# Adaptive-norm products: 28 of 36 streamed pieces move from TensorE to VectorE

## The chip, the cores and the metric

The kernel runs on one core of a Trainium2 chip. The metric is the device time of one execution in microseconds; the time before is the median of three runs.

## The reference, cut to what matters

The model is a two-layer trunk over 640 tokens (128 of context, 512 latent) with 1024 channels. Each layer first derives six modulation vectors of 1024 values from a conditioning vector, once for the context tokens (`c_ctx`) and once for the latent tokens (`c`):

```python
def adaln(cvec, w, b):
    m = jax.nn.silu(cvec) @ w + b          # (1024,) @ (1024, 6144)
    return jnp.split(m[:, None, :], 6, axis=-1)
...
sh1, sc1, g1, sh2, sc2, g2                  # the six parts, 0 to 5, in this order
h  = rmsnorm(x, g_norm1) * (1 + sc1) + sh1  # four mixers read h
x  = x + g1 * merged
h2 = rmsnorm(x, g_norm2) * (1 + sc2) + sh2
x  = x + g2 * (square(relu(h2 @ w_fc1)) @ w_fc2)
```

The rest of a layer (an SSD mixer, an S5 mixer, differential attention, windowed attention, gates, an output projection) is not touched by the change.

## The kernel before, in words

The activations stand transposed, channels on the 128 partitions and the 640 tokens along the free axis, in two halves of 320 tokens. A large product is split into three float32r products (high by high, low by high, high by low: lines 222, 223 and 224), so a dense block of 1024 inputs by 128 outputs takes 24 matrix products of 320 columns for each half. `load_w` brings a 512-column panel of weights (buffer `wr`, four slots), ScalarE copies it to its high part `wh` (line 211), and VectorE or, every third time, GpSimd subtracts to make the low part `wl` (line 195). The PSUM buffer of a dense half is `dn`, two slots. In the first product of the feed-forward block (`w_fc1`) ScalarE applies the ReLU (line 1742) and VectorE multiplies by `dn` again (line 1743), which frees the slot; in `w_out` and `w_fc2` VectorE adds the half to `x` (line 1537).

A modulation piece is a pair (part, q): 256 of the 6144 outputs. `adaln` computes it on TensorE: eight float32 products with the 32-column conditioning tile `cpad` as stationary operand and 256 columns of `w_mod` moving (line 287, each of them two records in the trace), four of them into each row group of one PSUM tile; a ScalarE copy to `mrow` (line 292); four products with `sel` that add the row groups and transpose (line 294); and one VectorE addition of the bias into `mods` (line 297). `make_gsc` (lines 341, 342) makes the gain of a norm out of part 1 or part 4.

Layer 0's parts 0, 1 and 2 are made in the prologue (buffers `wm`). The other 36 pieces are streamed by `adaln_ahead`, which loads each piece as four blocks of 256 KB into the ring `wa` (eight slots of 512 columns) and gives its products a higher scheduling priority. Layer 0's parts 3 and 4 (eight pieces) run in the output projection `w_out` of layer 0 (`PLAN["ad_out"]`). The rest is a generator `bgen` stepped by `between()`, five steps for every eight dense blocks of layer 0's feed-forward block: part 5 of layer 0 (four pieces), parts 0 and 1 of layer 1 (eight), the S5 matrices of layer 1 (`s5_build`, nine steps), parts 2 to 5 of layer 1 (sixteen). Layer 1's feed-forward block has no background work. The mid norm (`norm` with `PLAN["mid"]`) stands between `w_out` and `w_fc1`; its factor is a chain of small VectorE operations (`rsqrt`, lines 173 to 185), and its application is line 388 and line 400.

A scheduler orders the instructions of each engine and queue at build time with a simulated timeline; on the chip each engine and queue runs its list in that order. All `wr` and `wa` loads are issued by the SP queue.

Of the kernel before, what the change touches and what calls it, by code (L numbers as in the profile page):

```python
# [13 lines left out]
F32 = mybir.dt.float32  # L14
# [3 lines left out]
AF = mybir.ActivationFunctionType  # L18
ALU = mybir.AluOpType
# [4 lines left out]
D = 1024  # L24
# [18 lines left out]
NTAIL = 3  # L43

RINGS = dict(
    t1=3, tx=4, tq=6, ty=2, tw=5, td=5, nt=4, wa=8, wr=4, wh=4, wl=4, fh=10,
)

ENG = dict(
# [26 lines left out]
def hybrid_body(ctx: ExitStack, tc: tile.TileContext, a: dict, o: dict, dbg: dict):  # L76
    nc = tc.nc
    sp = nc.sync
# [7 lines left out]
    dp = ctx.enter_context(tc.tile_pool(name="dp", bufs=1, space=DRAM))  # L86
# [50 lines left out]
    def ring(tag, cols, where="pool"):  # L137
        def get(shape, name, dt=F32):
            n = int(np.prod(shape[1:]))
            t = top[where].tile([128, cols], dt, tag=tag, name=nm(name), bufs=RINGS[tag])[:, :n]  # L140
            if len(shape) == 2:
                return t
            letters = "abcdef"[: len(shape) - 1]
            dims = dict(zip(letters, shape[1:]))
            return t.rearrange(f"p ({' '.join(letters)}) -> p {' '.join(letters)}", **dims)

        return get
# [3 lines left out]
    t1, tx, tq = ring("t1", 320), ring("tx", 652), ring("tq", 256)  # L151
    ty, tw, td = ring("ty", 1024, "right"), ring("tw", 648, "right"), ring("td", 640, "right")

    nt, wa = ring("nt", 320), ring("wa", 512)

    def big(shape, tag, dt=F32, bufs=1, where="pool"):

        return top[where].tile(list(shape), dt, tag=tag, name=nm(tag), bufs=bufs)
# [116 lines left out]
    nc.vector.tensor_scalar(out=csg, in0=cth, scalar1=0.5, scalar2=0.5, op0=ALU.mult, op1=ALU.add)  # L275
    nc.vector.tensor_tensor(out=cpad[:, :, 0:2], in0=cs, in1=csg, op=ALU.mult)

    def adaln(l, parts, q, acc, out, raw, ks=range(KT)):

        n = len(parts)
        for i, part in enumerate(parts):
            for n_, k in enumerate(ks):
                r0 = 32 * (k % 4)
                c0 = (k % 2) * 256
                nc.tensor.matmul(  # L287
                    acc[r0:r0 + 32, i * 256:i * 256 + 256], cpad[:, k, :], raw(part, k // 2)[:, c0:c0 + 256],
                    start=(n_ < 4), stop=(n_ >= 4),
                )  # L290
        row = big([128, 512], "mrow", bufs=2) if n > 1 else t1([128, 256], "mrow")
        nc.scalar.copy(out=row, in_=acc[:, :n * 256])
        for j in range(2 * n):
            nc.tensor.matmul(out[:, 2 * j:2 * j + 2], row[:, j * 128:(j + 1) * 128], sel, start=True, stop=True)
        for i in range(n):
            f0 = parts[i] * 8 + q * 2
            nc.vector.tensor_tensor(
                out=mods[l][:, f0:f0 + 2, :],
                in0=out[:, 4 * i:4 * i + 4].rearrange("p (f s) -> p f s", s=2),
                in1=bmod[l][:, f0:f0 + 2].unsqueeze(2).to_broadcast((128, 2, 2)),  # L300
                op=ALU.add,
            )

    def adaln_ahead(l, parts, after=()):

        for part in parts:
            for q in range(4):
                halves = {}

                def raw(part, n, q=q, halves=halves):  # L310
                    if n not in halves:
                        halves[n] = wa([128, 512], "wa")
                        sp.dma_start(
                            out=halves[n], in_=a["w_mod"][l, part * 4 + q, n // 2][:, (n % 2) * 512:(n % 2) * 512 + 512]
                        )
                    return halves[n]


                for n in range(KT // 2):
                    raw(part, n)  # L320
                acc = mx()
                with tc.high_priority(offset=VISIT):
                    adaln(l, [part], q, acc[:, 0], acc[:, 1], raw, range(KT)[::-1])
                if q == 3 and part in after:
                    make_gsc(l, after[part])
                yield
# [8 lines left out]
    mods = [const(f"mod{l}", [128, 48, 2]) for l in range(L)]  # L335
# [137 lines left out]
    def s5_build(l, where, after):  # L473
# [114 lines left out]
            return x32[:, g0:g0 + 4].unsqueeze(2).to_broadcast((128, 4, n))  # L588

        def cmul(out, xr, yr, xi, yi, op, shape):  # L590
            u, v = big(shape, "s5u", bufs=2, where=where), big(shape, "s5v", bufs=2, where=where)
            nc.vector.tensor_tensor(out=u, in0=xr, in1=yr, op=ALU.mult)
            nc.gpsimd.tensor_tensor(out=v, in0=xi, in1=yi, op=ALU.mult)
            nc.vector.tensor_tensor(out=out, in0=u, in1=v, op=op)
# [964 lines left out]
    with tc.tile_pool(name="pro", bufs=1, reuse_waits="tile") as pool:  # L1559
        top["pool"] = pool  # L1560
        x = big([128, KT, T], "x")
        acc_n = big([128, T], "acc_n")
        h = h_tiles("h")

        accs, rb = mx(), mx()
        us = [big([128, 8, NI], "us0", bufs=2) for _ in range(2)]
        evs = [s5_store(u) for u in us]
        sums = [[dn(), dn()], [pb1(), None]]
        ws = []

        def panel_adaln(parts, q, acc, out):
            w = {part: [big([128, 1024], "wm", bufs=WM) for _ in range(2)] for part in parts}
            for part in parts:
                for i in range(2):
                    sp.dma_start(out=w[part][i], in_=a["w_mod"][0, part * 4 + q, i])
            if soon:
                load_all(soon)
                soon.clear()
            adaln(0, parts, q, acc, out, lambda part, n: w[part][n // 2][:, (n % 2) * 512:(n % 2) * 512 + 512])

        for q in range(5):
            if q < 4:
                panel_adaln((0, 1), q, accs[:, q % 2], rb[:, 0, HF + 8 * q:HF + 8 * q + 8])
                make_gsc(0, 0, 2 * q, 2)
            if q == 0:
                for k in range(KT):
                    sp.dma_start(out=x[:, k], in_=x_d[:, k])
                    for hf in range(2):
                        square_into(acc_n, x, k, hf)
                for hf in range(2):  # L1590
                    norm_spread(norm_factor(acc_n, hf)[0], rb, hf)
                sums[1][1] = pa()
                norms = [norm_mod(0, 0, x, rb, hf, *h) for hf in range(2)]
                continue
            for hf in range(2):
                step(norms[hf], 2)
            if q < 3:
                ws.append(load_ws(a["w_u"][0, q - 1], ahead=0))
            for k in {2: range(4), 3: range(4, 6), 4: range(6, 8)}.get(q, ()):
                for w, ps in zip(ws, sums):  # L1600
                    for hf in range(2):
                        mm3_step(ps[hf][:, :HF], split_w(w, k), hsl(h, k, hf), k == 0, k == KT - 1)
        for ev, ps, u, d in zip(evs, sums, us, u_d):
            for hf in range(2):
                ev(hf, ps[hf][:, :HF])
            nc.scalar.dma_start(out=d, in_=u)
        accs = mx()
        for q in range(4):
            panel_adaln((2,), q, accs[:, 0, (q % 2) * 256:], accs[:, 1, 8 * q:8 * q + 8])
        load_all(late)  # L1610
        maskf = t1([128, 2, 128], "mask")
        sp.dma_start(out=maskf, in_=a["wmask"])
        nc.vector.tensor_copy(out=maskb, in_=maskf)
        nc.vector.tensor_copy(out=identb, in_=ident)
        build_after[0] = h[1][0:1, KT - 1, T - 1:T].bitcast(F32)
        step(s5gen)
        adgen = adaln_ahead(0, range(3, 6), {4: 1})

    for l in range(L):
        acc_d = [dp.tile([128, T], F32, name=f"acc{l}_{f}") for f in range(KT)]  # L1620
# [92 lines left out]
        with ExitStack() as mlp:  # L1713
# [44 lines left out]
                )  # L1758

            norm(l, 1, x, acc_n, *h2, PLAN["mid"], tail, head)  # L1760
            bgen = [adgen]
            if l + 1 < L:
                bgen += [
                    adaln_ahead(l + 1, (0, 1), {1: 0}),
                    s5_build(l + 1, "mlp", lambda: act0[7][1][0:1, 0, T - 1:T].bitcast(F32)),
                    adaln_ahead(l + 1, range(2, 6), {4: 1}),
                ]
            bgen = itertools.chain(*bgen)

# [50 lines left out]
def _col(v):  # L1820

    v = np.asarray(v)
    return np.swapaxes(v.reshape(v.shape[:-1] + (v.shape[-1] // 128, 128)), -1, -2)


def _pack(inp):
# [3 lines left out]
    for n, s in sizes.items():  # L1830
# [9 lines left out]
    p = {}  # L1840
    st = np.stack
    p["x_t"] = np.concatenate([inp["x_prompt"][0], inp["x_sample"][0]], 0).T.reshape(KT, 128, T).transpose(1, 0, 2)
    p["c_t"] = np.stack([_col(inp["c_ctx"]), _col(inp["c"][0])], -1)
    p["w_mod"] = st([
        st([
            w.reshape(2, 4, 128, 24, 256)[s, :, :, q].transpose(1, 0, 2).reshape(128, 1024) for q in range(24) for s in range(2)
        ]).reshape(24, 2, 128, 1024) for w in inp["w_mod"]
    ])
    p["b_mod"] = _col(inp["b_mod"])
    p["g_norm"] = st([_col(inp["g_norm1"]), _col(inp["g_norm2"])], 2)  # L1850
    p["w_u"] = st([_fm(w[:, cols["u"]]) for w in w_in])
# [124 lines left out]
```

## Time and profile before

| what | value |
|---|---|
| median of 3 runs | 3039.33 us (3037.92 to 3041.75) |
| the profiled execution's own time | 3044.03 us |
| its span in the profile | 3042.2 us |
| TensorE products busy | 2847.3 us (94%) |
| TensorE weight loads busy | 2675.0 us (88%) |
| VectorE busy | 1734.1 us (57%) |
| ScalarE busy | 1183.8 us (39%) |
| GpSimd busy | 951.7 us (31%) |

Engines run in parallel, so the shares don't add up to one; the matrix products are pipelined and their ends are modelled, so a product's own duration is longer than its step in a row of products. The profiled execution took 1.8 us outside of its span.

### The profile page before, as it was taken

Reading aid. Unit: us, or ns where it says so; the run is one execution under the profiler, and the core shown is the slowest. Engines: PE = TensorE matmul, PEld = TensorE weight load, DVE = VectorE, ACT = ScalarE, POOL = GpSimd, SP = SyncE. Lnnn points to the kernel's source line nnn. Section 1 sums busy time; section 2 is a strip of 40 time slices with the busy share of each in tenths; the row PEclk is TensorE's granted clock in tenths of the full one; section 3 lists DMA queues with packets and bytes.
Section 4 is the critical chain, followed back from the end, with each engine's and each line's share of the span. In section 5 each row is a group of like instructions: output and inputs, shape, how many; then the busy total and the mean of one; then the engine's idle time right before and its main releaser. Section 6 shows DMA issues by size and latency. Waiting matters only on the chain.

```text
span 3042.2 us, 54194 instructions
## 1 busy us (share of the span) xinstructions
PE 2847.3 (94%) x20782; PEld 2675.0 (88%) x20782; DVE 1734.1 (57%) x3826; ACT 1183.8 (39%) x2660; POOL 951.7 (31%) x1058
## 2 busy tenths in 40 slices
PE   8778898998899999999999889999999999999999
PEld 6768887798689988999999879888997999999999
DVE  6977936756543556556235686576666436433333
ACT  5234463244344342323234536523534434322323
POOL 1656504613220312334111570264131122211111
PEclk9889898999899999999999999989999999999999
DMA  8453253223432735444443323432252323222222
GB/s 287 155 188 109 73 151 100 81 81 115 144 126 68 238 105 180 134 136 162 146 151 119 126 87 111 137 107 61 91 177 89 105 84 119 63 74 74 76 77 84
DMA packets 240707, 364.22 MB, mean 120 GB/s; under 512 B 42144, under 2 KB 104352, under 8 KB 240448
## 3 DMA queue, kind: packets, MB, share of 16 engines
q1 hardware_dynamic: 225696, 336.97, 35.5%
q10 hardware_dynamic: 14752, 23.78, 2.1%
q8 instruction: 164, 2.69, 0.4%
q14 instruction: 95, 0.78, 0.1%
HBM read 294.98 MB, written 65.68 MB: 119 GB/s over the span
## 4 chain that ended last, share of the span: by engine, by line
PE 69%; DVE 15%; issue 3%; DMA 3%; POOL 2%; ACT 2%; SPq 1%; DVEq 0%; ACTq 0%; POOLq 0%
PE dn L222 19%; PE dn L223 19%; PE dn L224 19%; DVE wl L195 1%; DVE B L757 1%; PE mx L287 1%; PE mx L1277 1%; PE pb L1321 1%; PE mx L1315 1%; PE mx L1451 1%; DVE sc L754 1%; DMA sseg<-acum 1%; PE mx L1406 1%; DVE sc L755 1%; PE mx L735 1%
## 5 line engine op out<-in xcount | busy, mean ns | idle before, releaser
L195 POOL TENSOR_TENSOR wl<-wr,wh 128x512 fp32r<-128x512 f32 x207 | 280.9, 1357 | 1241.2 <-ACT wh L211 1153.1
L211 ACT CAST wh<-wr 128x512 fp32r<-128x512 f32 (+1 forms) x614 | 378.6, 621 | 599.1 <-PE dn L223 531.5
L195 DVE TENSOR_TENSOR wl<-wr,wh 128x512 fp32r<-128x512 f32 (+1 forms) x407 | 318.3, 785 | 306.1 <-ACT wh L211 295.4
L224 PE MATMUL dn<-hh,wl 128*128 128x320 f32 x1328 | 422.4, 318 | 11.6 <-DVE wl L195 11.6
L222 PE MATMUL dn<-hh,wh 128*128 128x320 f32 x1328 | 426.4, 321 | 4.9 <-ACT gah L1479 3.1
L223 PE MATMUL dn<-hl,wh 128*128 128x320 f32 x1328 | 424.8, 320 | 2.4 <-DVE hl L400 2.4
L222 PE MATMUL dn<-fh,wh 128*128 128x320 f32 x1008 | 313.9, 311 | 2.3 <-DVE x L1537 2.3
L222 PE MATMUL dn<-nh,wh 128*128 128x320 f32 x992 | 311.1, 314 | 3.7 <-DVE r L1743 3.7
L224 PE MATMUL dn<-fh,wl 128*128 128x320 f32 x1008 | 313.7, 311 | 0.0
L223 PE MATMUL dn<-fl,wh 128*128 128x320 f32 x1008 | 313.1, 311 | 0.0
L223 PE MATMUL dn<-nl,wh 128*128 128x320 f32 x992 | 308.8, 312 | 3.9 <-DVE nl L400 1.6
L224 PE MATMUL dn<-nh,wl 128*128 128x320 f32 x992 | 307.6, 310 | 0.0
L223 PE MATMUL dn<-wl,hh 128*128 128x256 f32 (+1 forms) x880 | 256.6, 293 | 17.4 <-DVE wl L195 15.0
L224 PEld LDWEIGHTS dn<-hh,wl 128*128 128x128 f32 x1328 | 257.5, 194 | 15.3 <-DVE wl L195 12.7
L222 PEld LDWEIGHTS dn<-hh,wh 128*128 128x128 f32 x1328 | 257.6, 194 | 12.9 <-ACT gah L1479 4.3
L222 PE MATMUL dn<-wh,hh 128*128 128x256 f32 (+1 forms) x880 | 258.9, 296 | 10.6 <-ACT hsq L1184 4.5
L223 PEld LDWEIGHTS dn<-hl,wh 128*128 128x128 f32 x1328 | 257.7, 194 | 7.4 <-DVE hl L400 3.5
L224 PE MATMUL dn<-wh,hl 128*128 128x256 f32 (+1 forms) x880 | 255.2, 291 | 0.0
L222 PE MATMUL dn<-B,wh 128*128 128x320 f32 x640 | 207.8, 326 | 16.4 <-ACT B L824 5.7
L1537 DVE SCALAR_TENSOR_TENSOR x<-dn,mod,x 128x192 f32<-128x192 f32 (+2 forms) x240 | 98.0, 436 | 212.1 <-PE dn L224 203.9
L223 PE MATMUL dn<-B,wh 128*128 128x320 f32 x640 | 203.3, 318 | 0.9 <-DVE B L195 0.9
L224 PE MATMUL dn<-B,wl 128*128 128x320 f32 x640 | 201.1, 314 | 0.0
(403 smaller groups left out, 6725.9 us busy)
## 6 DMA issues: line engine op xcount, KB each, us to landing
wr<-in_w_fc_dram SPq DMA_DIRECT2D x256, 256.0 KB, 2.8
wa<-in_w_mod_dram SPq DMA_DIRECT2D x144, 256.0 KB, 4.4
wr<-in_w_gate_dram SPq DMA_DIRECT2D x128, 256.0 KB, 2.9
wr<-in_w_tok_dram SPq DMA_DIRECT2D x80, 256.0 KB, 2.9
wr<-in_w_branch_dram SPq DMA_DIRECT2D x64, 256.0 KB, 3.0
acc<-gth SPq DMA_DIRECT2D x48, 320.0 KB, 3.0
gold<-acc SPq DMA_DIRECT2D x48, 320.0 KB, 3.2
wm<-in_w_mod_dram SPq DMA_DIRECT2D x24, 512.0 KB, 6.8
```

The costliest lines, as they stand in the source:

```text
L195: engine.tensor_tensor(out=out, in0=full, in1=hi, op=ALU.subtract)
L211: nc.scalar.copy(out=hi, in_=raw)
L222: nc.tensor.matmul(ps, sh, vh, start=first, stop=False)
L223: nc.tensor.matmul(ps, sh, vl, start=False, stop=False)
L224: nc.tensor.matmul(ps, sl, vh, start=False, stop=last)
L287: nc.tensor.matmul(acc[r0:r0 + 32, i * 256:i * 256 + 256], cpad[:, k, :], raw(part, k // 2)[:, c0:c0 + 256], start=(n_ < 4), stop=(n_ >= 4),)
L735: nc.tensor.matmul(xs[:, ri, g * NI:(g + 1) * NI], pm[:, ri, g * 128:(g + 1) * 128], U[:, g0 + g], start=True, stop=True)
L754: ve.tensor_tensor(out=pair[:, 0], in0=src, in1=re.to_broadcast(shp), op=ALU.mult)
L755: ve.tensor_tensor(out=pair[:, 1], in0=src[:, :, ::-1], in1=im.to_broadcast(shp), op=ALU.mult)
L757: ve.tensor_tensor(out=dst, in0=dst, in1=pair[:, i], op=ALU.add)
L1277: nc.tensor.matmul(sc[:, n, c0:c0 + (k1 - k0) * 128], qT[rows[n], g, ct], kT[rows[n], k0:k1].rearrange("p k c -> p (k c)"), start=True, st ...
L1537: nc.vector.scalar_tensor_tensor(out=xs, in0=ps[:, c0:c1], scalar=mods[l][:, part * 8 + f, s:s + 1], in1=xs, op0=ALU.mult, op1=ALU.add)
```

## The change

Twenty-eight pieces leave TensorE: part 5 of layer 0, and all six parts of layer 1. The host lays their weights out by output (`w_modt`: for each block of 128 outputs one tile of 128 partitions by 1024 inputs). For each such block and each of the two conditioning vectors VectorE multiplies the tile by the vector, repeated on all partitions, and sums along the row, with the bias as start value; the sum goes straight to `mods`. A piece has two blocks, so four such operations; the products go to a PSUM tile of the ring `mx` that nobody reads. The conditioning vectors, after their SiLU, are written once to DRAM in the prologue (`c_d`) and read back onto all partitions once in each layer (`cb`). Part 5 of layer 1 moves from layer 0's to layer 1's feed-forward block. The ring `wa` has three slots of 1024 columns instead of eight of 512, for the eight remaining pieces as well. In the feed-forward block the scratch tiles `s5u` and `s5v` of `s5_build` have one slot each instead of two. The background generator of layer 0 has 33 steps instead of 37.

```diff
-    t1=3, tx=4, tq=6, ty=2, tw=5, td=5, nt=4, wa=8, wr=4, wh=4, wl=4, fh=10,
+    t1=3, tx=4, tq=6, ty=2, tw=5, td=5, nt=4, wa=3, wr=4, wh=4, wl=4, fh=10,
...
-    nt, wa = ring("nt", 320), ring("wa", 512)
+    nt, wa = ring("nt", 320), ring("wa", 1024)
...
+    cr = tmp([128, 16], "cr", bufs=1)
+    sp.dma_start(out=cr, in_=a["c_rows"])
+    crt = tmp([128, 16], "crt", bufs=1)
+    nc.scalar.activation(out=crt, in_=cr, func=AF.Tanh, scale=0.5)
+    nc.vector.tensor_scalar(out=crt, in0=crt, scalar1=0.5, scalar2=0.5, op0=ALU.mult, op1=ALU.add)
+    nc.vector.tensor_tensor(out=cr, in0=cr, in1=crt, op=ALU.mult)
+    c_d = dp.tile([128, 16], F32, name="c_d")
+    sp.dma_start(out=c_d, in_=cr)
...
                 def raw(part, n, q=q, halves=halves):
-                    if n not in halves:
-                        halves[n] = wa([128, 512], "wa")
-                        sp.dma_start(
-                            out=halves[n], in_=a["w_mod"][l, part * 4 + q, n // 2][:, (n % 2) * 512:(n % 2) * 512 + 512]
-                        )
-                    return halves[n]
+                    if n // 2 not in halves:
+                        halves[n // 2] = wa([128, 1024], "wa")
+                        sp.dma_start(out=halves[n // 2], in_=a["w_mod"][part * 4 + q, n // 2])
+                    return halves[n // 2][:, (n % 2) * 512:(n % 2) * 512 + 512]
...
+    def cond_rows():
+
+        cb = big([128, 2, D], "cb")
+        sp.dma_start(out=cb.rearrange("p s k -> p (s k)"), in_=c_d.rearrange("a b -> (a b)").unsqueeze(0).to_broadcast((128, 2 * D)))
+        return cb
+
+    def adaln_rows(l, parts, cb, after=()):
+
+        for part in parts:
+            for q in range(4):
+                for f in range(part * 8 + 2 * q, part * 8 + 2 * q + 2):
+                    w = wa([128, D], "wa")
+                    sp.dma_start(out=w, in_=a["w_modt"][l * 48 + f - 40])
+                    prod = mx().rearrange("p a b -> p (a b)")
+                    for s in range(2):
+                        nc.vector.tensor_tensor_reduce(
+                            out=prod, in0=w, in1=cb()[:, s], scale=1.0, scalar=bmod[l][:, f:f + 1], op0=ALU.mult,
+                            op1=ALU.add, accum_out=mods[l][:, f, s:s + 1],
+                        )
                 if q == 3 and part in after:
                     make_gsc(l, after[part])
                 yield
...
-            u, v = big(shape, "s5u", bufs=2, where=where), big(shape, "s5v", bufs=2, where=where)
+            u, v = (big(shape, t, bufs=2 if where == "build" else 1, where=where) for t in ("s5u", "s5v"))
...
-        adgen = adaln_ahead(0, range(3, 6), {4: 1})
+        adgen = adaln_ahead(0, (3, 4), {4: 1})
...
             norm(l, 1, x, acc_n, *h2, PLAN["mid"], tail, head)
-            bgen = [adgen]
+            cb = cond_rows()
+            bgen = [adgen, adaln_rows(l, (5,), lambda: cb)]
             if l + 1 < L:
                 bgen += [
-                    adaln_ahead(l + 1, (0, 1), {1: 0}),
+                    adaln_rows(l + 1, (0, 1), lambda: cb, {1: 0}),
                     s5_build(l + 1, "mlp", lambda: act0[7][1][0:1, 0, T - 1:T].bitcast(F32)),
-                    adaln_ahead(l + 1, range(2, 6), {4: 1}),
+                    adaln_rows(l + 1, range(2, 5), lambda: cb, {4: 1}),
                 ]
```

## Rows read from the trace of the kernel before

**Rows 1.** The page's busy times: span, busy us, share, instructions.

```profile
span 3042.2 us, 54194 instructions
...
PE 2847.3 (94%) x20782; PEld 2675.0 (88%) x20782; DVE 1734.1 (57%) x3826; ACT 1183.8 (39%) x2660; POOL 951.7 (31%) x1058
```

**Rows 2.** The page's chain of work that ended last, by engine.

```profile
PE 69%; DVE 15%; issue 3%; DMA 3%; POOL 2%; ACT 2%; SPq 1%; DVEq 0%; ACTq 0%; POOLq 0%
```

**Rows 3.** Windows, layer 0: length, busy PE PEld DVE ACT POOL, PEclk, DMA, GB/s.

```profile
1017.00:1110.00 93.00, 90.27 (x653) 79.65 (x652) 46.94 (x124) 32.00 (x73) 13.44 (x12) 0.96 0.62 210
1110.00:1625.00 515.00, 505.68 (x3944) 477.07 (x3944) 266.16 (x586) 156.17 (x322) 139.47 (x130) 0.99 0.45 144
```

**Rows 4.** Waits of the TensorE instructions, 1110 to 1625 us: total, times, longest.

```profile
PE dn L222 <- DVE r L1743: 4.3, 5, 1.4
PE mx L287 <- DMA wa<-in_w_mod_dram: 2.5, 2, 2.0
```

**Rows 5.** TensorE timeline around one piece: start, us, instruction.

```profile
1271.04 0.31 PE L222 MATMUL dn<-nh,wh 128*128 128x320 f32 x1
1271.28 1.07 PE L287 MATMUL mx<-wa,cpad 128*32 128x256 f32 x16
1272.28 0.41 PE L223 MATMUL dn<-nl,wh 128*128 128x320 f32 x1
1272.54 0.31 PE L224 MATMUL dn<-nh,wl 128*128 128x320 f32 x1
...
1283.58 0.31 PE L222 MATMUL dn<-nh,wh 128*128 128x320 f32 x1
1283.72 0.50 PE L294 MATMUL mx<-sel,mrow 128*128 128x2 f32 x4
1284.08 0.40 PE L223 MATMUL dn<-nl,wh 128*128 128x320 f32 x1
```

**Rows 6.** Windows of line 287 alone, then of line 294 alone, same stretch.

```profile
1110.00:1625.00 515.00, 30.77 (x432) 12.05 (x432) 0.99 0.45 144
...
1110.00:1625.00 515.00, 14.29 (x112) 15.13 (x112) 0.99 0.45 144
```

**Rows 7.** VectorE by source line, two-input operations: ns minimum/median/maximum; last row: total us, mean.

```profile
L195 DVE TENSOR_TENSOR wl<-wr,wh x407: 677/693/1783, 23.1 to 3023.1; 128x512 fp32r<-128x512 f32 x135, 128x544 fp32r<-128x544 f32 x1
L195 DVE TENSOR_TENSOR fl<-r,fh x88: 479/493/1407, 1108.2 to 2984.0; 128x320 fp32r<-128x320 f32 x88
L901 DVE SCALAR_TENSOR_TENSOR cv<-xp,cw,cv x72: 876/893/1922, 286.3 to 1906.2; 128x646 f32<-128x646 f32 x72
L1033 DVE TENSOR_TENSOR sseg<-sseg,scb x20: 678/1519/1777, 494.5 to 2056.9; 128x512 f32<-128x512 f32 x20
...
L195 DVE TENSOR_TENSOR wl<-wr,wh 128x512 fp32r<-128x512 f32 x403 | 315.0, 785 | 306.1 <-ACT wh L211 295.4 <-PE dn L224 5.6 <-DMA pm<-s5p 3.2
```

**Rows 8.** Windows as in rows 3: a dense stretch of `s5_build`; layer 1's mid norm.

```profile
1344.00:1362.00 18.00, 18.00 (x165) 17.76 (x165) 16.15 (x28) 3.96 (x7) 10.48 (x10) 1.00 0.50 157
2555.00:2605.00 50.00, 45.70 (x309) 43.35 (x307) 37.37 (x95) 25.08 (x57) 11.12 (x12) 1.00 0.19 60
```

**Rows 9.** ScalarE and VectorE timelines: one half of `w_fc1` is evacuated.

```profile
1135.49 0.44 ACT L1742 ACTIVATE r<-dn 128x320 f32<-128x320 f32 x1 [1.48 <-PE dn L224]
...
1135.96 0.49 DVE L1743 TENSOR_TENSOR r<-r,dn 128x320 f32<-128x320 f32 x1 [1.43 <-ACT r L1742]
```

**Rows 10.** DMA issues: number, KB each, median us from issue to landing.

```profile
wa<-in_w_mod_dram SPq DMA_DIRECT2D x144, 256.0 KB, 4.4
...
wm<-in_w_mod_dram SPq DMA_DIRECT2D x24, 512.0 KB, 6.8
```

**Rows 11.** Bias additions in `w_out` of layer 0; first norm application on VectorE's timeline.

```profile
L297 DVE TENSOR_TENSOR mod<-mx,bmod x8: 161/162/164, 1030.5 to 1071.3; 128x4 f32<-128x4 f32 x8
...
1088.02 2.42 DVE L388 SCALAR_TENSOR_TENSOR nh<-x,gsc,mx 128x128 f32<-128x128 f32 x8 [0.81 <-PE mx L371]
```

**Rows 12.** Timeline of the first microseconds: VectorE ends the conditioning vector.

```profile
2.85 0.18 DVE L276 TENSOR_TENSOR cpad<-cs,csg 128x16 f32<-128x16 f32 x1
```

More of the change, by code (lines that the diff above doesn't have):

```diff
@@ L323, in adaln_ahead @@
                     adaln(l, [part], q, acc[:, 0], acc[:, 1], raw, range(KT)[::-1])
+                if q == 3 and part in after:
+                    make_gsc(l, after[part])
+                yield
+    def cond_rows():
[14 more added lines that the diff above has]
+                        )
                 if q == 3 and part in after:
@@ L1574, in panel_adaln @@
                 for i in range(2):
-                    sp.dma_start(out=w[part][i], in_=a["w_mod"][0, part * 4 + q, i])
+                    sp.dma_start(out=w[part][i], in_=a["w_mod"][part * 4 + q, i])
             if soon:
@@ L1843, in _pack @@
     p["c_t"] = np.stack([_col(inp["c_ctx"]), _col(inp["c"][0])], -1)
+    p["c_rows"] = np.stack([inp["c_ctx"], inp["c"][0]]).reshape(128, 16)
+    w = inp["w_mod"][0].reshape(2, 4, 128, 24, 256)
     p["w_mod"] = st([
[L1845 to L1848, printed above, removed]
+        w[s, :, :, q].transpose(1, 0, 2).reshape(128, 1024) for q in range(20) for s in range(2)
+    ]).reshape(20, 2, 128, 1024)
+    p["w_modt"] = np.concatenate([inp["w_mod"][0].T.reshape(48, 128, D)[40:], inp["w_mod"][1].T.reshape(48, 128, D)])
     p["b_mod"] = _col(inp["b_mod"])
```

## The prediction

> **What bounds the kernel now.** I read the page's busy times first, then its chain of work, then windows over the stretch that holds the pieces. TensorE is the full engine and VectorE has 43% of the span free [rows 1]; 69% of the chain that ended last runs over TensorE, 15% over VectorE [rows 2]. The windows say it for the place of the change. Of the 28 pieces that move, 27 run their products from 1110 to 1625 us, under layer 0's feed-forward block: line 287 has 432 records there, sixteen for each piece [rows 6]. [...] What TensorE waits for is small: 4.3 us for VectorE to free a `dn` slot, 2.5 us for the piece's own weights [rows 4]. So a microsecond taken from TensorE's list there comes off the end, as long as the list is fed. The 28th piece ran its products just ahead, in the mid norm, where TensorE is 97% busy [rows 3].
>
> **What the change removes.** The dense products start every 0.14 to 0.15 us (1283.58 to 1283.72 [rows 5]). Around the eight products of a piece the start of one dense product to that of the next is 1271.04 to 1272.28, 1.24 us, so 1.09 more than the pace, and the dense product behind it takes 0.26 instead of 0.15, another 0.11: 1.20 us. The four `sel` products take 1283.58 to 1284.08, 0.35 over the pace, and 0.11 again: 0.46 us [rows 5]. Together 1.66 us for a piece, 28 x 1.66 = 46.5 us. The windows bound it from the other way: 30.77 + 14.29 = 45.1 us with such an instruction in flight [rows 6]. I take -46.5; the ends are -45 and -49 (with the 2.5 us of waits for weights). The ScalarE copies and the VectorE bias additions also go, both off the path; the additions took 0.16 us each [rows 11].
>
> **What it adds on VectorE.** 28 pieces x 4 = 112 multiply-and-sum operations over 1024 columns, 96 in layer 0 (24 pieces), 16 in layer 1. No operation of the kernel before multiplies and sums on VectorE at once, and none of VectorE's writes PSUM, so the price is bounded from near rows. Two float32 inputs from SBUF take 493 ns for 320 columns and 693 ns for 512 [rows 7]: 1.04 ns a column, so 1.23 us for 1024, the low end. While GpSimd works on the same memory, 512 columns can take 1519 ns [rows 7], 2.2 times as long: 2.69 us, the high end. The mean of all 403 subtractions of 512 columns is 785 ns against the usual 693 [rows 7], a factor of 1.13; GpSimd is 27% busy in this stretch [rows 3], so I take 1.23 x 1.13 = 1.39 us. The three-operand form of line 901 speaks for the near end: 893 ns for 646 columns, where the slope gives 833 [rows 7].
>
> [...]
>
> 96 x 1.39 = 133 us; less 24 additions of 0.16, VectorE holds 266 + 133 - 4 = 395 us of a stretch that has shrunk to 515 - 46.5 = 468: 84%. It is not the bound. The question is what its queue now delays. Where `s5_build` fills it, 16.15 of 18 us, 90%, TensorE still runs 18.00 of 18 [rows 8]; that stretch is `w_fc2`, whose half is evacuated by VectorE alone. Under `w_fc1` a half needs ReLU and multiplication, 1135.49 to 1136.45, 0.96 us [rows 9], while the next half lasts 24 steps of 0.14 to 0.15, 3.5 us: 2.5 us to spare. One operation of 1.39 us ahead of line 1743 fits; two (2.8) cost 0.3 us, three 1.7. About half of the 24 pieces fall under `w_fc1`, at 1.6 dense blocks a step some 40 halves. One in five with a wait of 1 us gives **+8 us**; the ends are 0 and 30 (three in four wait). Behind a waiting sum on VectorE stand the `wl` subtractions; they have the four slots of `wl`, two dense blocks, ahead of TensorE. A sum that waits for its own weights stops them too: the loads took 4.4 us for 256 KB and 6.8 us for 512 KB in the busy prologue [rows 10], and three slots hold six sums, 8.3 us of work, so the next tile lands in time.
>
> **The mid norms.** Part 5's sixteen operations come first in the generator, so they can fall into the mid norm, among the dependent small operations of `rsqrt` and line 388. Layer 0: first application at 1088.02 [rows 11]; layer 1: VectorE busy 37.4 and TensorE 45.7 of 50 us [rows 8]. An engine's list is fixed, so one that was put into the chain delays it by 1.39 us whole. Low end 0; high end 16 x 1.39 = 22 us in each of the two, if all were there. I take 2 us each, **+4**: loads that come three at a time, and dense halves that TensorE does in between, speak for the low end.
>
> **The ring of the eight pieces left.** Three slots of 512 KB hold one and a half pieces, where eight of 256 KB held two. Before, the pieces came every (1071.3 - 1030.5)/7 = 5.8 us [rows 11]. With 6.8 us for a load [rows 10] and some 2 us until TensorE takes it, 1.5 pieces every 8.8 us are 5.9 us a piece: the last one is done within a microsecond or two of where it was, with 17 us to the first application. But TensorE's order is fixed, and a late load now stops it directly. **+2**; ends 0 and 12 (1.5 us for each piece).
>
> **The rest.** With one slot for `s5u` and `s5v`, GpSimd's product waits for VectorE's sum of the one before, and the next sum for it; in 32 large products at about 1.6 us that is at most 53 us of idle VectorE, which has 468 - 395 = 73. **+1**; ends 0 and 10, where TensorE's transposes stand behind. In the prologue the second vector adds a tanh, two small VectorE operations and two issues of SP, one of which waits for the product; the first vector was ready at 2.85 + 0.18 us [rows 12]. If SP's list has that store in front of the first weights, they start about 3 us later; behind them it costs nothing: **+0.5**; ends 0 and 3. The broadcast of `cb`, 1 MB a layer, is hidden: DMA is busy 62% in the stage before its use [rows 3]. If that cover fails, the first sums wait some 7 us, and the four pieces aren't needed until the residuals of `w_fc2`, five dense blocks of 7 us later. The bytes of the pieces themselves stay the same.
>
> **Sum.** -46.5 + 8 + 4 + 2 + 1 + 0.5 = -31 us against the profiled execution's own 3044.0 (span 3042.2 and 1.8 around it) is 3013; this execution lay 4.7 above the median of the runs, so as a median **3008 us**.
>
> **Rivals.** First, on the other side: the sum runs at half rate. Then it takes 2 x 1.23 x 1.13 = 2.77 us, and VectorE needs 262 + 96 x 2.77 = 528 us where TensorE needs 468: it sets the pace, 60 us over. -46.5 + 60 + 7.5 = +21: 3060 us. VectorE is full from (468 - 262)/96 = 2.14 us on, and the gain is gone at about 2.5. For it speaks that no row has the operation; against it the three-operand row. [...]
>
> Second, the order inside the lists eats the gain: the two norms take most of their high end (30 us together) and the ring 9 of its 12: -46.5 + 8 + 30 + 9 + 1.5 = +2, so 3041 us, no measurable change. For it speaks that the mid norms are the places where TensorE has idle time (4.3 of 50 us [rows 8]); against it that the operations have no raised priority, and 32 of 112 are concerned.
>
> Third, VectorE's queue costs nothing (rows 8 hold under `w_fc1` too): -46.5 + 2 = -44, 2995 us.
>
> That the change doesn't free TensorE at all is hardly possible; the products are gone.
>
> **How the numbers follow.** A measurement of this kernel can tell about 0.2%, 6 us, from no change. The likeliest case, stalls between 0 and 30 us around -31, has 0.55, and its own range is 2998 to 3026; the third rival has 0.18, the second 0.12, the first 0.10, and 0.05 stays for order effects further on, of either sign. Faster: 0.55 + 0.18 + 0.02 = 0.75; same: most of the second, 0.09; slower: 0.16. The range reaches from the third rival's low end to just above the second: 2988 to 3045; the half rate stays outside.
>
> **What would show it.** Right: lines 287 and 294 keep only the prologue's and eight pieces' records; 112 operations on VectorE near 1.3 to 1.4 us; VectorE near 84% and TensorE still above 96% in layer 0's feed-forward stretch, which ends some 35 us earlier; the waits of `dn` for line 1743 grow from 4 to about 12 us. Wrong: an operation of 2.5 us or more; the feed-forward stretch as long as before with TensorE below 92%; the norm at 1088 us of before coming 10 us later; products of line 287 waiting for `wa`.

## The result, and the profile after

The changed kernel took 3072.85 us (median of 4 runs, 3068.89 to 3073.09) against 3038.81 for the kernel before beside it: 1.0104 times as long, 95% interval 1.0088 to 1.0120. The forecast was 3008, with a range that ended at 3045. The profiled execution's span is 3071.0 us, 28.8 more than before; by the medians the difference is 34.0 us, because the profiled execution of the kernel before (3044.03 us) lay 5.2 us above its median. What follows reads the 28.8 us.

The page's busy times after; they answer to [rows 1]:

```profile
span 3071.0 us, 53136 instructions
...
PE 2813.7 (92%) x20222; PEld 2665.0 (87%) x20222; DVE 1874.0 (61%) x4024; ACT 1170.4 (38%) x2633; POOL 956.9 (31%) x1058
```

TensorE is indeed busy for 34 us less, and VectorE for 140 us more; still, the span grew. So TensorE has more idle time, and the question is where. The first and last start of some products divide the span. In the changed kernel, by line 222's products (durations minimum/median/maximum in ns, then first and last start in us):

```profile
L222 PE MATMUL dn<-mh,wh x224: 305/309/614, 1017.3 to 2584.0; 128*128 128x320 f32 x112
...
L222 PE MATMUL dn<-nh,xh x32: 306/312/636, 1126.3 to 2637.4; 128*128 128x320 f32 x32
...
L222 PE MATMUL dn<-fh,wh x1008: 305/309/417, 1199.7 to 3066.8; 128*128 128x320 f32 x168
L222 PE MATMUL dn<-fh,xh x16: 309/309/394, 1628.3 to 1644.3; 128*128 128x320 f32 x16
```

The first `mh` product opens layer 0's output projection; the first product with `xh` weights after `nh` stands at the end of the mid norm; the first with `fh` opens `w_fc2`; the first `fh,xh` is the tail of layer 0; the last `mh` and the last `nh,xh` enclose layer 1's mid norm. The stages, for all kernels of this study, are differences of such starts in each profiled execution (us):

| kernel | A: to `w_out` of layer 0 | B: `w_out`, mid norm | C: first `w_fc1` | D: to layer 0's tail | E: layer 1 to its mid norm | F: layer 1's mid norm | G: rest | span |
|---|---|---|---|---|---|---|---|---|
| before | 1015.1 | 91.0 | 57.0 | 454.9 | 956.4 | 34.0 | 433.8 | 3042.2 |
| after | 1017.3 | 109.0 | 73.4 | 428.6 | 955.7 | 53.4 | 433.6 | 3071.0 |
| paced | 1017.0 | 91.9 | 52.5 | 428.3 | 951.6 | 35.5 | 433.7 | 3010.5 |
| gate | 1013.7 | 88.2 | 59.3 | 452.4 | 950.2 | 33.9 | 438.9 | 3036.6 |
| gate in layer 1 | 1014.8 | 108.3 | 71.7 | 429.8 | 955.0 | 34.0 | 440.1 | 3053.7 |
| no sums | 1009.3 | 96.5 | 57.2 | 418.8 | 949.0 | 36.5 | 433.1 | 3000.4 |
| small buffers, before | 1016.7 | 87.8 | 57.0 | 460.8 | 956.0 | 34.0 | 434.0 | 3046.3 |
| no sums, two slots | 1012.1 | 94.5 | 59.6 | 415.6 | 951.9 | 36.6 | 433.7 | 3004.0 |
| spread | 1006.7 | 89.8 | 52.5 | 422.7 | 952.5 | 34.0 | 433.7 | 2991.9 |
| spread, two slots | 1012.6 | 90.3 | 52.6 | 419.8 | 954.8 | 34.0 | 433.6 | 2997.7 |

Stage A lies ahead of nearly all that differs and yet goes from 1006.7 to 1017.3, E from 949.0 to 956.4: some us of a span are scatter there, so I read the other stages, and whole times by their ratios. D gives back 26.3 us; B loses 18.0, C 16.4 and F 19.4.

The windows of these stages in the changed kernel (length; busy time of PE and PEld, the products and weight loads of TensorE, of DVE, which is VectorE, of ACT, ScalarE, and of POOL, GpSimd; granted clock as a share of full speed; DMA share; GB/s) answer to [rows 3] and [rows 8]; the first begins with the tail of `w_out`:

```profile
1069.00:1126.00 57.00, 33.60 (x220) 30.86 (x219) 48.94 (x120) 16.73 (x43) 6.83 (x6) 0.79 0.48 162
1126.00:1200.00 74.00, 58.66 (x341) 56.45 (x341) 72.98 (x119) 23.55 (x51) 17.29 (x12) 0.88 0.55 176
1200.00:1628.00 428.00, 406.33 (x3039) 399.30 (x3038) 290.19 (x593) 125.09 (x246) 126.89 (x119) 0.99 0.39 127
...
2584.00:2637.00 53.00, 34.40 (x191) 32.58 (x191) 48.17 (x104) 20.81 (x49) 10.57 (x10) 0.77 0.26 86
```

In the two mid norms TensorE is busy for 59% and 65%, VectorE for 86% and 91%; in the first blocks of `w_fc1` VectorE has 73.0 of 74 us. The waits of TensorE there, 1060 to 1205 us and then 2580 to 2660 us (total, times, longest), answer to [rows 4]:

```profile
PE mx L402 <- DVE ry L185: 15.1, 1, 15.1
PE dn L222 <- DVE r L1774: 13.6, 6, 5.7
PE dn L223 <- DVE nl L431: 5.1, 3, 4.6
...
PE mx L402 <- DVE ry L185: 13.1, 2, 12.4
PE dn L223 <- DVE nl L431: 4.2, 1, 4.2
```

Line 402 spreads the norm factor (line 371 of the kernel before); it waits for `rsqrt`'s last operation. VectorE's timeline over the second half's factor in layer 0 shows why. Each of its dependent operations of 0.15 us is followed by a sum (line 351) and the read of its accumulator:

```profile
1107.22 0.15 DVE L173 TENSOR_SCALAR rv<-pa 80x4 f32<-80x4 f32 x1
1107.30 1.85 DVE L351 CUSTOM_DVE_ANT_0 mx<-wa,cb,bmod 128x1024 f32<-128x1024 f32 x1
1109.07 0.13 DVE L351 DVE_READ_ACCUMULATOR2_ANT mod<- 128x1 f32 x1
1109.07 0.16 DVE L175 TENSOR_SCALAR ri<-rv 80x4 int32<-80x4 int32 x1
1109.24 1.29 DVE L351 CUSTOM_DVE_ANT_0 mx<-wa,cb,bmod 128x1024 f32<-128x1024 f32 x1
1110.45 0.14 DVE L351 DVE_READ_ACCUMULATOR2_ANT mod<- 128x1 f32 x1
1110.45 0.16 DVE L177 TENSOR_SCALAR rg<-ri 80x4 int32<-80x4 int32 x1
1110.62 1.29 DVE L351 CUSTOM_DVE_ANT_0 mx<-wa,cb,bmod 128x1024 f32<-128x1024 f32 x1
1111.83 0.14 DVE L351 DVE_READ_ACCUMULATOR2_ANT mod<- 128x1 f32 x1
1111.83 0.15 DVE L181 TENSOR_TENSOR rs<-rg 80x4 f32<-80x4 f32 x1
...
1124.31 0.15 DVE L185 SCALAR_TENSOR_TENSOR ry<-rb,ry 80x4 f32<-80x4 f32 x1
```

That isn't chance on the chip: VectorE's list, as the build wrote it, has the same order. Eleven sums stand between the twelve operations, in layer 0 and again in layer 1. The last operation of the chain starts at 1124.31, 17.1 us after the first; in the kernel before the same chain took 2.8 us (1098.41 to 1101.16):

```profile
1098.41 0.15 DVE L173 TENSOR_SCALAR rv<-pa 80x4 f32<-80x4 f32 x1
...
1101.16 0.16 DVE L185 SCALAR_TENSOR_TENSOR ry<-rb,ry 80x4 f32<-80x4 f32 x1
```

And the sums by source line (durations in ns, what VectorE's idle time before them waited for in us):

```profile
L351 DVE CUSTOM_DVE_ANT_0 mx<-wa,cb,bmod x112: 1272/1284/2326, 1085.9 to 2619.7; 128x1024 f32<-128x1024 f32 x112
L351 DVE DVE_READ_ACCUMULATOR2_ANT mod<- x112: 129/136/146, 1087.1 to 2620.9; 128x1 f32 x112
...
  DMA wa<-in_w_modt_dram: 2.8, 6
```

The price of a sum is as forecast, and its weights are hardly waited for. It is the place of the sums in VectorE's list that cost the time.

### The profile page after: what moved, and what is told of

The parts are those of the page before. It is cut to its first block, busy times and chain, and to the rows that moved or that the text cites. A ratio compares the mean times of both kernels' runs of the same rounds, so it can differ in the third digit from the quotient of the medians.

```text
span 3071.0 us, 53136 instructions
## 1 busy us (share of the span) xinstructions
PE 2813.7 (92%) x20222; PEld 2665.0 (87%) x20222; DVE 1874.0 (61%) x4024; ACT 1170.4 (38%) x2633; POOL 956.9 (31%) x1058
## 4 chain that ended last, share of the span: by engine, by line
PE 42%; DVE 13%; issue 4%; POOL 3%; DMA 3%; ACT 1%; SPq 0%; DVEq 0%; POOLq 0%; ACTq 0%
PE dn L222 12%; PE dn L223 12%; PE dn L224 12%; DVE mx L351 3%; DMA wa<-in_w_modt_dram 1%; DVE wl L195 1%; POOL s5v L624 1%; DMA sseg<-acum 1%; DVE B L788 1%; DVE nh L419 1%; PE mx L1308 1%; PE pb L1352 1%; PE mx L1437 1%; PE mx L1346 0%; DVE sc L786 0%
## 5 line engine op out<-in xcount | busy, mean ns | idle before, releaser
L222 PEld LDWEIGHTS dn<-nh,wh 128*128 128x128 f32 x992 | 191.0, 193 | 27.4 <-DVE r L1774 23.7
```

Source lines behind the costliest of these rows:

```text
L222: nc.tensor.matmul(ps, sh, vh, start=first, stop=False)
```

## The experiments

Two theories went into the first four runs. (The evacuation of a dense half is the VectorE operation that reads it out of its `dn` slot.) Order: the time is lost because sums stand between the small operations of the norm factor, and in runs ahead of line 1774 (1743 of before), so that TensorE waits. Room: the sums cost their time wherever they stand.

**Paced.** Each piece's sums are listed behind the evacuation of the dense block traced just ahead of them (`tc.issue_after`).

```diff
+                    with tc.issue_after(evac[0].ins):
                         for s in range(2):
                             nc.vector.tensor_tensor_reduce(
...
-                nc.vector.tensor_tensor(out=r, in0=r, in1=ps, op=ALU.mult)
+                evac[0] = nc.vector.tensor_tensor(out=r, in0=r, in1=ps, op=ALU.mult)
...
-            nc.vector.scalar_tensor_tensor(
+            evac[0] = nc.vector.scalar_tensor_tensor(
                 out=xs, in0=ps[:, c0:c1], scalar=mods[l]...
```

> The changed kernel, but each piece's sums are listed on VectorE behind the evacuation of the dense block traced just ahead of them; nothing else differs. Order theory: the 52 us lost in the two mid norms and in the first dense blocks come from sums listed between the small operations of the norm factor and in runs ahead of line 1774; so nearly all comes back and the time is 3005 us (2995 to 3020). Rival, room theory: the 153 us of sums cost TensorE their time wherever they stand (a full VectorE, or sums and GpSimd slowing each other); then it stays at 3055 to 3080 us.

Measured: 3011.59 us, 0.9906 of before (0.9883 to 0.9929), inside the range of the order theory. The same 112 sums, loads and buffers, 0.9906 in place of 1.0104. Its window of stage D, and then TensorE's largest wait in it:

```profile
1161.00:1590.00 429.00, 406.66 (x3048) 399.97 (x3047) 352.93 (x693) 124.90 (x247) 135.59 (x119) 0.99 0.48 157
```

```profile
PE dn L222 <- DVE r L1777: 19.4, 10, 4.8
```

VectorE is 82% busy there, more than in the changed kernel, and the stage isn't longer (428.3 against 428.6). Room is refuted; against the changed kernel B gives back 17.1 us, C and D 21.2, F 17.9, and E, where nothing differs, 4.1: nearly all of the 60.5 us between the spans.

Stage C shows a price that I had not counted, the clock. Both kernels have the same products there (338 and 337 in the windows of the stage). TensorE is without one for 15.3 us in the changed kernel and 2.4 in the paced; but the products are also in flight longer, 58.1 us against 50.1, at a granted clock of 0.88 against 1.00. So of the 20.9 us between the two, 12.9 are waits and 8.0 go with the lower clock behind them.

**Gate.** The repeated vectors may be loaded only when the mid norm's last low part is written, so no sum can run in a mid norm. Behind it their order is the scheduler's.

```diff
-    def cond_rows():
+    def cond_rows(late):
...
+        nc.gpsimd.tensor_copy(out=cb[0:1, 0, 0:1], in_=late)
...
-            cb = cond_rows()
+            cb = cond_rows(h2[1][0:1, KT - 1, T - 1:T].bitcast(F32))
```

> The changed kernel, but the repeated vectors are loaded only once the mid norm's last low part is written, so no sum can run in a mid norm; their order behind it is left to the scheduler. Order theory: the two norms' losses (25 and 19 us against the kernel before) go, some of the 16 us in the first dense blocks may stay: 3020 us (3005 to 3035). Room theory: 3055 to 3080 us.

Measured: 3043.26 us, 1.0012 (0.9998 to 1.0027). The norms are cured, 88.2 and 33.9 us, as the order theory says; but the time missed my 3020 by 23, and the range by 8. The sums that may not stand in the norm now crowd stage D, 452.4 us. Windows of its start, and TensorE's waits over the stage, then in layer 1 behind the mid norm:

```profile
1161.00:1230.00 69.00, 63.39 (x412) 61.71 (x411) 69.00 (x138) 14.01 (x25) 13.63 (x8) 0.98 0.62 203
1230.00:1300.00 70.00, 60.92 (x391) 58.66 (x392) 69.16 (x130) 22.33 (x47) 16.68 (x11) 0.98 0.59 192
```

```profile
PE dn L222 <- DVE r L1775: 22.6, 13, 4.5
PE dn L222 <- DVE x L1569: 12.1, 8, 3.2
...
PE dn L222 <- DVE r L1775: 3.2, 1, 3.2
```

VectorE is full (69.00 of 69 us) although it idles later in the same stage (busy for 29.52 of the 70 us from 1440 on): I read this as gaps that the scheduler filled with sums of 1.28 us, weights being up to three tiles ahead, so that the evacuations come late. So the runs are a second loss beside the norms: C and D take 511.7 us here and 480.8 in the paced kernel, 31 us for the order alone.

**Gate in layer 1 only.**

```diff
-            cb = cond_rows(h2[1][0:1, KT - 1, T - 1:T].bitcast(F32))
+            cb = cond_rows(h2[1][0:1, KT - 1, T - 1:T].bitcast(F32) if l else None)
...
-        nc.gpsimd.tensor_copy(out=cb[0:1, 0, 0:1], in_=late)
+        if late is not None:
+            nc.gpsimd.tensor_copy(out=cb[0:1, 0, 0:1], in_=late)
```

> The same gate in layer 1 only; layer 0 as in the changed kernel. Order theory: only layer 1's mid norm changes, 53 us back to 34, so 3073 - 19 = 3054 us (3048 to 3060), with layer 0's part as in the changed kernel. Room theory: no change, 3068 to 3078 us.

Measured: 3049.05 us, 1.0033 (1.0018 to 1.0048), inside the range of the order theory, and 0.7% or 22 us better than the changed kernel by the ratios. F is back at 34.0 us from 53.4, G takes 440.1 instead of 433.6, where the sixteen sums now run behind the norm (in the gate run TensorE waits 3.2 us there for an evacuation); B and C are those of the changed kernel. The mid norm of layer 1 alone gave back 19 us, of which G took 6.5.

**No sums.** Each sum is replaced by an addition of one column; the modulation values of the 28 pieces are not computed.

```diff
-                    prod = mx().rearrange("p a b -> p (a b)")
                     for s in range(2):
-                        nc.vector.tensor_tensor_reduce(
-                            out=prod, in0=w, in1=cb()[:, s], scale=1.0, scalar=bmod[l][:, f:f + 1], op0=ALU.mult,
-                            op1=ALU.add, accum_out=mods[l][:, f, s:s + 1],
+                        nc.vector.tensor_tensor(
+                            out=mods[l][:, f, s:s + 1], in0=w[:, s:s + 1], in1=bmod[l][:, f:f + 1], op=ALU.add,
                         )
```

> The changed kernel without the sums: each is replaced by an addition of one column, so that the modulation values of the 28 pieces are not computed; loads, rings and all else stay. It gives what TensorE's relief is worth with VectorE left alone. Both theories: 3039 - 46.5 + a few us for the smaller ring, 2996 us (2988 to 3005). If it is above 3010, the relief was mis-sized or the rings cost more than thought.

Measured: 3007.51 us, 0.9896 (0.9869 to 0.9924), 11 us above what I expected and just outside my range. C and D take 476.0 us against 511.9 before: 35.9 us of relief, not 46.5. The paced kernel is 4 us above this one, inside the intervals: well placed, the sums cost next to nothing. What makes B and F longer here than before (96.5 and 36.5 us, with no sum in them) stays open. TensorE still waited for line 1774's operation (1772 here), from 1061 to 1582 us:

```profile
PE dn L222 <- DVE r L1772: 14.0, 8, 4.0
```

so the next runs asked what cut the relief: the smaller buffers, or my count.

**Small buffers in the kernel before.** Three `wa` slots of 1024 columns, one slot for `s5u` and `s5v`; all pieces on TensorE.

```diff
-    t1=3, tx=4, tq=6, ty=2, tw=5, td=5, nt=4, wa=8, wr=4, wh=4, wl=4, fh=10,
+    t1=3, tx=4, tq=6, ty=2, tw=5, td=5, nt=4, wa=3, wr=4, wh=4, wl=4, fh=10,
...
-            u, v = big(shape, "s5u", bufs=2, where=where), big(shape, "s5v", bufs=2, where=where)
+            u, v = (big(shape, t, bufs=2 if where == "build" else 1, where=where) for t in ("s5u", "s5v"))
```

> The kernel before with the change's smaller buffers alone: three slots of 1024 columns for the streamed pieces, one slot each for the two scratch tiles of the S5 matrices in the feed-forward block; all 36 pieces stay on TensorE. If these buffers are what cuts the relief from the 46.5 us forecast to the 34 us that the run without sums gave, this is 8 to 14 us slower than before; if the relief itself was mis-sized, it is within 4 us of it.

Measured: 3049.7 us, 1.0038 (1.0025 to 1.0052): 11.6 us by the ratio, inside the 8 to 14 that speak for the buffers. D is 5.9 us longer; the spans differ by 4.1 only, so where the rest of the 11.6 lies isn't shown. From 1000 to 1630 us TensorE never waits for a `wa` load in this run; it waits 10.1 us for the multiplication (line 1741 here), against 4.3 before. Against this kernel the run without sums gains 517.8 - 476.0 = 41.8 us in C and D, and 11.6 + 31.6 = 43.2 by the ratios. So the buffers took some 6 us or more; by these runs the count was 3 to 5 us high, which the intervals don't tell from right.

**No sums, two slots.** As "no sums", with a second slot for the scratch tile that GpSimd writes.

```diff
-            u, v = (big(shape, t, bufs=2 if where == "build" else 1, where=where) for t in ("s5u", "s5v"))
+            u, v = (big(shape, t, bufs=2 if where == "build" or t == "s5v" else 1, where=where) for t in ("s5u", "s5v"))
```

> The run without sums, with a second slot for the scratch tile that GpSimd writes. In that run TensorE waited some 9 us for line 1743's multiplication of before while the S5 matrices were made under the first feed-forward product. If the single slot causes that, 8 us come back: 4% of a thousandth less than 3000 us, about 2999; if not, within 3 us of the run without sums.

Measured: 3003.43 us, 0.9879 (0.9855 to 0.9903). The intervals overlap, and C and D take 475.2 us where they took 476.0: that the slot brings 8 us back isn't shown. What makes TensorE wait there stays open.

**Spread.** Two sums behind each evacuated half, instead of four behind a dense block.

```diff
+    def row_sums(l, f, w, cb, gsc, ins):
+        prod = mx().rearrange("p a b -> p (a b)")
+        with tc.issue_after(ins.ins):
+            for s in range(2):
+                nc.vector.tensor_tensor_reduce(
...
+    def evacuated(ins):
+        if pend:
+            pend.pop(0)(ins)
```

(`adaln_rows` loads the tile and puts the call into `pend`; the ends of `squares` and `residual` call `evacuated` with their VectorE instruction.)

> As the paced kernel, but two sums behind each evacuated half instead of four behind a dense block. If the 19 us that TensorE still waits for the multiplication of an evacuated half in the paced kernel come from four sums in a row, half of it goes: 10 us below the paced kernel, ratio to before 0.987. If they come from the S5 matrices, it equals the paced kernel, 0.990.

Measured: 3006.5 us, 0.9887 (0.9854 to 0.9920). C and D take 475.2 us, 5.6 less than paced, about the half of what I expected, and as much as without sums; the intervals of the two ratios overlap, so that spread beats paced isn't shown by the times. TensorE's wait for the multiplication, 1000 to 1630 us:

```profile
PE dn L222 <- DVE r L1785: 15.2, 11, 2.6
```

against 21.6 us in the paced kernel over the same stretch, and 14.0 without sums.

**Spread, two slots.** The spread kernel with the second slot of `s5v`, as in the diff above.

> The spread kernel with the second scratch slot of the S5 matrices. If both the order and the slot count, 6 to 8 us below the spread kernel, ratio to before 0.984 to 0.985; it would be the fastest version. If the slot is of no account, as the spread kernel.

Measured: 2999.11 us, 0.9867 (0.9846 to 0.9889), the lowest median of all; C and D take 472.4 us. Whether it beats "spread" is inside the intervals; that it beats both kernels, by 1.3% and 2.3%, is not.

## Why the prediction was wrong

**The bound** was read rightly. TensorE's list was what set the end in layer 0's feed-forward block: with the sums left out, C and D shrink by 35.9 us.

**What the change removes**, -46.5: 41.8 in C and D and 43.2 by the ratios (small buffers, with and without the products). The step of 1.66 us a piece was taken around one undisturbed piece; the mechanism was right, and the size by these runs 7 to 10% too high.

**The price of a sum**, 1.39 us: 1.385 in the mean of all 112, and 0.14 for the accumulator's read that I had not counted. The first rival, half rate, needed 2.77; that the measured time lies near its 3060 us is no sign for it. No run shows the factor of two that this rival rests on: the median sum took 1284 ns for 1024 columns, where a halving would make some 2460, an estimate from the 1.23 us of the slope. The trace records the sum as CUSTOM_DVE_ANT_0.

**Late evacuations**, +8: the changed kernel takes 502.0 us in C and D, 26.0 more than without sums, part of it the lower clock (0.88 in stage C, 0.97 there without sums). TensorE waits 28.0 us there for the multiplication, where I had forecast some 12. I spread the sums evenly over the stage, one step each 1.6 blocks, because the generator is stepped so. That is the order of tracing, not that of VectorE's list: the list has them far ahead of it. 55 of the 96 had run by 1200 us, when the first `w_fc2` block began, and full stretches of VectorE (busy for 29.6 of 30 us from 1200 on) stand next to half-empty ones (48.0 of 128 us from 1500 on). The 84% that I computed was near as a mean (80% over C and D in the paced kernel, 82% in D) and said nothing of the order.

**The mid norms**, +4: this step failed worst. They cost 18.0 (stage B) and 19.4 us (F). The second rival had the mechanism and the place, with 22 us as the high end for each; I took 2, arguing that loads come three at a time and that the sums have no raised priority. Neither protected this chain, and TensorE had no dense half left to do in between: it ran no product for 15.1 us. Nor were sixteen sums the limit in layer 0; nineteen had started by 1127 us. The loads took 3.7 us to land:

```profile
wa<-in_w_modt_dram SPq DMA_DIRECT2D x56, 512.0 KB, 3.7
```

A tile has two sums, so a tile each 2.8 us was enough to fill every gap. That the scheduler puts a low operation wherever no higher one is ready at that instant, as between two dependent operations, is my reading of the list; no run tests that rule by itself. The windows of TensorE over that wait add the clock to the price (length, busy, granted clock, DMA share, GB/s):

```profile
1105.00:1110.00 5.00, 4.39 (x30) 1.00 0.30 105
1110.00:1115.00 5.00, 0.00 (x0) 0.75 0.39 129
1115.00:1120.00 5.00, 0.00 (x0) 0.50 0.50 179
...
1125.00:1130.00 5.00, 5.00 (x23) 0.54 0.49 162
```

When the next block begins, after the 15 us without a product, the granted clock is 0.50 (in windows of 1 us from 1126 to 1129 us; 1.00 again from 1130 to 1131): from 1126.66 us on ten of its products start 0.27 us apart instead of 0.15.

**The smaller buffers**, +2 and +1: 5.9 us in D, where I had put 1; which of the two buffers it is isn't shown. The last of the eight pieces left did not delay the norm: B is 87.8 us with the small buffers and 91.0 before. **The prologue**, +0.5: SP's list has the store behind the first weights, the better of my two cases; the eight `x` loads are issued from 6.35 us on instead of 5.18. A is 2.2 us longer, inside its scatter, so the half microsecond can't be told.

```profile
1.65 1.85 SPq L1606 DMA_DIRECT2D wm<-in_w_mod_dram  x4
3.71 0.34 SPq L286 DMA_DIRECT2D c_d<-cr  x1
```

The sum as measured: -41.8 (relief) + 5.9 (buffers) + 26.0 (order under the feed-forward block) + 18.0 + 19.4 (mid norms) + 1.3 (stages A, E, G) = +28.8 us. Each term is the difference of one execution of each kernel.

The chances were wrong as well: the second rival had 0.12, with 30 us for the norms, 8 for late evacuations and 9 for the ring of the eight pieces. Norms and runs together came to 63, and the ring, by the run with small buffers, nothing ahead of the norm. With the order mended the forecast comes near: -31 us are 0.990 of before, and the paced kernel measured 0.9906.

## What to carry to other kernels

A filler of more than a microsecond on an engine that also runs chains of short dependent operations must be told where to stand: here the build's order put a sum between each two of them, and the chain paid each filler whole, 17.1 us in place of 2.8. A mean load below 100% (here 61% of the span) is no proof that an engine has room: look at who may run in which gap, and tie background work to an event of the foreground (here: behind each evacuation, 0.9887 instead of 1.0104). When a change moves work to another engine, price the smallest chain that it can get into, number of links times the length of the moved operation, before the sum of the work.

## What the runs showed of the hardware

A multiply-and-sum of 1024 float32 columns on VectorE, with products to PSUM, is two entries in the trace: 1284 ns and an accumulator read of 136 ns (medians of 112). The 81 sums with no GpSimd instruction in flight beside them took 1272 to 1296 ns, the other 31 took 1278 to 2326: the longest, from 1216.24 us on, ran together with a GpSimd subtraction of 2.11 us from 1215.36. In the kernel before, five of the twenty operations of line 1033 had no GpSimd instruction beside them and took 678 to 685 ns; the other fifteen took 678 to 1777.
